# Six of eight output tiles of the last down-projection group as three seven-product pairs, and two changes of order around them

## The chip, the cores and the metric

The kernel runs on one core of a Trainium2 chip. The metric is the time of one execution on the device in microseconds; of several executions the median is given. Five engines work beside each other, each through its own queue in order: PE (TensorE, matmuls; its weight loads are listed as PEld), DVE (VectorE), ACT (ScalarE), POOL (GpSimd; here it issues DMAs that add while they copy) and SP (SyncE, which issues the ordinary DMAs).

## The reference

One decoder layer over 512 tokens of width 1024: an RMS norm, one wide input projection, a pooling mixer and a sparse attention whose results are merged by gates, an output projection with a residual, then a second norm and a gated feed-forward part. What the change touches, cut to the core:

```python
blk = kv[:, idx] + pe[None, None, :, None, :]           # compression: windows of 32 tokens
hid = silu(einsum('bnlgd,ldh->bngh', blk, w1))
...
h = rms_norm(x, ffn_norm_g)                              # x: (1, 512, 1024)
gate_pre, val = split(h @ w_up, 2)                       # D_FF = 2816 = 22 blocks of 128
gate_c = causal_dwconv(gate_pre, conv_w, conv_b)         # width 3 along the tokens
x = x + (silu(gate_c) * val) @ w_down                    # y @ w_down, y: (512, 2816)
```

All is float32. The output is `x`, kept as eight tiles of 128 features by 512 tokens.

## The kernel before

**Precision.** A float32 matrix is split into a high part that PE takes in its fast format (`fp32r`) and the rest. A product is three matmuls: high by high, high by low, low by high. `mm3` (line 451) does this with 512 token columns, one unit of three matmuls per block of 128 of the contraction. The splits are ACT conversions and DVE subtractions (`split`), or, in `split_by_dma` (line 1112), two ACT conversions and a POOL DMA that adds.

**Feed-forward.** The up projection runs over 22 blocks `f`. In blocks 0 and 2 (`up_plain`) gate and value are two plain products of 8 units. The other 20 (`up_fast`, line 1246) compute gate and value together: with weights and tokens each cut in two halves, a two by two block product is made by seven half products (`product`, line 1196: 4 units of three matmuls with 256 columns) in place of eight. The sums of weight halves (`r1`, `r2`, `s3`, and sums in place in `wraw`) are made by DVE and split again; the sums of the tokens' halves (`th`, `tl`) are made once. The last two products of a block, for `h5` and `h4`, are held back and stand inside the next block. When they end, DVE and ACT make the block's gate, its convolution and `y`, and `split_y` splits `y` into `yh`, `yl`.

**Down projection.** It sums over the 22 blocks of `y`. Blocks 0 to 15 are four groups of four (`dn_group`); each group gives eight tiles of 12 matmuls, which are added to `x2`. These `dn` tiles stand between the up products where the table `FILL` (lines 56 to 58) says: an entry gives, for block `f`, how many stand before it and at three places in it. Groups become available at blocks 5, 9, 13 and 17 (`AT`). Blocks 16 to 21 of `y` are the last group, called `dz` here after its weights `wdz`: a loop over eight output tiles (line 1329), 6 units each, whose result plus `x2` is stored. The eighth tile is made as two halves of 256 columns.

**Compression.** `kv_in` (line 747) projects the inputs and DVE makes two tensors `kcb` by adding the position parameters. A `behind` at line 756 holds these additions until `turned[3]`, the last step of transposing queries and keys (`k`), has been done. PE then multiplies `kcb` with `w1`.

**Order.** The code doesn't issue instructions; it records them, and a planner (`Plan.run`, line 226; `emit`, line 375) writes an order for each engine. PE's work comes in two streams, each in its written order: the main line and, until the attention ends, a second one of projections, taken when the main line isn't ready. For the other engines the planner picks among what is ready by due times, which it works out back from PE. It tries several orders and keeps the one that it prices lowest. So an edit anywhere can reorder every queue. SBUF pages of 128x512 (`page`, 54 of them) and the three slots of each ring (`wraw`, `whi`, `wlo`) are handed on from user to user; a tile made by `soon` takes its page in the written order. Since all instructions leave through the planner, all have the line 394 in the profile, and are told apart by tiles: `mm`, `tr`, `av`, `sc` are the accumulator banks.

Of the kernel before, what the change touches and what calls it, by code (L numbers as in the profile page):

```python
# [9 lines left out]
F32R = mybir.dt.float32r  # L10
I32 = mybir.dt.int32
AF = mybir.ActivationFunctionType
# [3 lines left out]
P = 128  # L16
# [38 lines left out]
AT = (5, 9, 13, 17)  # L55
FILL = {f: (0, 0, 0, 0) for f in range(22)}
FILL.update({f: (0, 1, 1, 0) for f in range(5, 18)})
FILL.update({18: (0, 1, 0, 0), 19: (0, 1, 0, 0), 20: (0, 1, 0, 0), 21: (0, 1, 0, 0)})
TRIES = 12
RESERVE = 3  # L60
BASE = 5.0
# [336 lines left out]
def hybrid_layer(ctx: ExitStack, tc: tile.TileContext, xT, pos, par, cst, poolw, w1, wa, wb, wf,  # L398
# [15 lines left out]
    def soon(name, dt=F32):  # L414
        t = page(name, dt=dt)
        pl.early[t.tensor.name] = len(pl.early)
        return t
# [7 lines left out]
    def split(dst_hi, dst_lo, src, scale=None):  # L425
        if scale is None:
            ACT.activation(dst_hi, src, AF.Copy)
            DVE.tensor_sub(dst_lo, src, f32(dst_hi))
        else:
            ACT.activation(dst_hi, src, AF.Copy, scale=scale)  # L430
            DVE.scalar_tensor_tensor(dst_lo, src, scale, f32(dst_hi), op0=ALU.mult, op1=ALU.subtract)

    def ring(name, dt=F32):
        return pl.tile(sb, (P, 1024), dt, name, name, RINGS[name])
# [13 lines left out]
    def flat(ap):  # L448
        return ap.rearrange("p k n -> p (k n)")
# [252 lines left out]
    def qk_transpose(t):  # L702
        pt = bank("tr", (P, 4, P))
        with pl.unit():
            for i in range(4):
                PE.transpose(pt[:, i], qp[t][:, 2 * i:2 * i + 2].rearrange("p a d -> p (a d)"), ident)
        for a in range(2):
            QT[a, t] = page("qt", (P, 4, P), F32R)
            halves_of(pt, QT[a, t], QT[a, t], a)
        if t % 2:  # L710
            pt = bank("tr", (P, 2, 2, P))
            with pl.unit():
                for j in range(2):
                    for b in range(2):
                        PE.transpose(pt[:, j, b], kp[t - 1 + j][:, 2 * b:2 * b + 2].rearrange("p a d -> p (a d)"), ident)
            for g in range(2):
                x, y = (page("kt", (P, 2, 2, P), F32R) for _ in range(2))
                KT[g, t // 2, g], KT[1 - g, t // 2, g] = x, y
                r, o = halves_of(pt, x, x, g)
                ACT.activation(y[o], pt[r], AF.Copy)  # L720
                ACT.activation(y[r], f32(x[o]), AF.Copy)

    rotate(0)
    rotate(1)
    turned = []
    for t in range(NT):
        qk_transpose(t)
        turned.append(pl.last())
# [17 lines left out]
    with pl.on("f"):  # L746
        def kv_in(i):
            pt = feature(i, xh, xl)
            kc = page("kc", (P, 2, 256))
            for g in range(2):  # L750
                for q in range(2):
                    DVE.tensor_mul(kc[q * 64:(q + 1) * 64, g], pt[g * 64:(g + 1) * 64, q::2],
                                   rb[g * 64:(g + 1) * 64, q::2])
            for a in range(2):
                b = page("kcb", (P, 2, 32, 8))
                with pl.behind(turned[3]):
                    DVE.tensor_add(b.rearrange("p g n l -> p (g n) l"), kc.rearrange("p g (n l) -> p (g n) l", l=8),
                                   pe[:, i, 8 * a:8 * a + 8][:, None, :].to_broadcast([P, 64, 8]))
                KC[i, a] = b
# [314 lines left out]
    def any_bank():  # L1074
        turn[0] += 1
        return bank(("mm", "tr", "tr", "mm", "tr", "av")[turn[0] % 6])
# [35 lines left out]
    def split_by_dma(hi, lo, x):  # L1112
        ACT.activation(lo, x, AF.Copy, scale=-1.0)
        POOL.dma_start(lo, x, accum_op=ALU.add)
        ACT.activation(hi, x, AF.Copy)
# [42 lines left out]
    def conv(f, g, pg):  # L1158
# [4 lines left out]
        ACT.activation(t, t, AF.Silu)  # L1163
        return t

    def split_y(f, y):
        yh[f], yl[f] = page("yh", dt=F32R), page("yl", dt=F32R)
        split(yh[f], yl[f], y)

    def up_plain(f):  # L1170
        pts = []
# [20 lines left out]
    def back(x):  # L1192
        n = x.ap[1][1]
        return bass.AP(tensor=x.tensor, offset=x.offset + n - 1, ap=[list(x.ap[0]), [-1, n]])

    def product(bank_, a, b, k0):
        ah, al = a
        bh, bl = b
        for k in range(4):
            c = slice(k * P, (k + 1) * P)  # L1200
            with pl.unit():
                for j, (w, x) in enumerate(((ah, bh), (ah, bl), (al, bh))):
                    PE.matmul(back(bank_[:, :H2]), w[:, c], back(x(k)), start=k0 and k == 0 and j == 0,
                              stop=k == 3 and j == 2, skip_group_check=True)

    def mov(i, half):
        if i == 0:
# [35 lines left out]
            for a in range(2):  # L1243
                fills.append(lambda free, c=c, a=a: one(c, a, free))

    def up_fast(f, n1, n2, n3):
        rg, r1, r2 = ring("wraw"), soon("r1"), soon("r2")
        SP.dma_start(rg, flat(wup[f, 0]))
        with pl.behind(begun[-2 - max(0, 3 - f)]):
            SP.dma_start(r1, flat(wup[f, 1, :, 0:4]))  # L1250
            SP.dma_start(r2, flat(wup[f, 1, :, 4:8]))

        def pair():
            return soon("sh", F32R), soon("sl", F32R)

        def summed(x):
            lo, hi = soon("sl", F32R), soon("sh", F32R)
            split_by_dma(hi, lo, x)
            return hi, lo

        a1 = ring("whi", F32R), ring("wlo", F32R)
        split(*a1, rg)
        halves_ = lambda a, i: tuple(q[:, i * 512:(i + 1) * 512] for q in a)
        s3 = soon("s3")
        DVE.tensor_add(s3, rg[:, :512], r1)
        h5 = summed(r2)
        DVE.tensor_add(r1, r1, r2)
        h3 = summed(s3)
        DVE.tensor_add(rg[:, :512], rg[:, :512], r1)
        h1 = summed(r1)  # L1270
        h2 = pair()
        split(*h2, rg[:, :512])
        DVE.tensor_add(rg[:, 512:], rg[:, 512:], rg[:, :512])
        h4 = summed(rg[:, 512:])
        bx, by, bq = any_bank(), any_bank(), any_bank()
        half = [page("u1")]
        u2, u3 = half[0][:, :H2], half[0][:, H2:]
        g, y = page("fg"), page("y")
        product(bx, halves_(a1, 0), mov(0, 0), True)
        begun.append(pl.last())  # L1280
        ACT.activation(by[:, :H2], bx[:, :H2], AF.Copy)
        more = list(held)
        del held[:]
        if more:
            more[0]()
        else:
            product(bq, h1, mov(2, 0), True)
        fill(n1)
        product(by, h2, mov(2, 1), False)
        ACT.activation(u2, by[:, :H2], AF.Copy)  # L1290
        if more:
            more[1]()
        fill(n3)
        if more:
            product(bq, h1, mov(2, 0), True)
        product(bx, halves_(a1, 1), mov(1, 0), False)
        DVE.tensor_mul(g[:, :H2], bx[:, :H2], rb[:, :H2])
        fill(n2)
        product(by, h3, mov(3, 0), False)
        ACT.activation(u3, by[:, :H2], AF.Copy)  # L1300
        DVE.tensor_add(y[:, H2:], bq[:, :H2], u3)
        DVE.tensor_mul(y[:, H2:], y[:, H2:], rb[:, H2:])

        def end1():
            product(by, h5, mov(3, 1), False)
            DVE.tensor_mul(y[:, :H2], by[:, :H2], rb[:, :H2])

        def end2():
            product(bq, h4, mov(1, 1), False)
            DVE.tensor_add(g[:, H2:], bq[:, :H2], u2)  # L1310
            DVE.tensor_mul(g[:, H2:], g[:, H2:], rb[:, H2:])
            t = conv(f, g, g)
            DVE.scalar_tensor_tensor(y, y, -1.0, t, op0=ALU.mult, op1=ALU.mult)
            split_y(f, y)

        held.extend((end1, end2))
# [9 lines left out]
    fill(1, True)  # L1326
    finish()
    fill(9, True)
    for f in range(8):
        wh, wl = weights(flat(wdz[f]), 768, "v")  # L1330
        pt = any_bank()
        o = page("o")
        if f < 7:
            mm3(pt, wh, wl, yh, yl, 16, KF, koff=16, nk=KF, first=16)
            DVE.tensor_add(o, pt, x2[f])
            SP.dma_start(out[f], o)
            continue
        for h in range(2):
            s = slice(h * H2, (h + 1) * H2)
            pt = any_bank() if h else pt  # L1340
            for k in range(16, KF):
                c = slice((k - 16) * P, (k - 15) * P)
                with pl.unit():
                    for j, (w, q) in enumerate(((wh, yh), (wh, yl), (wl, yh))):
                        PE.matmul(back(pt[:, :H2]), w[:, c], back(q[k][:, s]), start=k == 16 and j == 0,
                                  stop=k == KF - 1 and j == 2)
            DVE.tensor_add(o[:, s], pt[:, :H2], x2[f][:, s])
            SP.dma_start(out[f, :, s], o[:, s])

    pl.emit(TRIES, RESERVE)  # L1350

# [92 lines left out]
```

## Time and profile before

| | |
|---|---|
| median of 3 runs | 691.0 us (690.94 to 691.12) |
| the profiled execution | 690.67 us |
| its span, first to last instruction | 688.9 us |
| granted TensorE clock | 1.000 |
| PE, DVE, ACT, POOL busy | 683.1, 502.6, 430.0, 100.2 us |
| DMA | 113.99 MB, mean 165 GB/s |

In a row of the chain stand start, length, engine, accumulator bank and the count of merged instructions, in microseconds from the start of the span. In a row of the timeline the operation is written output<-inputs, with the shape; a bracket gives the idle time before it and what ended it. A row of the groups gives busy time and mean nanoseconds of one, then idle time before and what ended most of it.

### The profile page before, as it was taken

Reading aid. Unit: us, or ns where it says so; the run is one execution under the profiler, and the core shown is the slowest. Engines: PE = TensorE matmul, PEld = TensorE weight load, DVE = VectorE, ACT = ScalarE, POOL = GpSimd, SP = SyncE. Lnnn points to the kernel's source line nnn. Section 1 sums busy time; section 2 is a strip of 40 time slices with the busy share of each in tenths; the row PEclk is TensorE's granted clock in tenths of the full one; section 3 lists DMA queues with packets and bytes.
Section 4 is the critical chain, followed back from the end, with each engine's and each line's share of the span. In section 5 each row is a group of like instructions: output and inputs, shape, how many; then the busy total and the mean of one; then the engine's idle time right before and its main releaser. Section 6 shows DMA issues by size and latency. Waiting matters only on the chain.

```text
span 688.9 us, 11345 instructions
## 1 busy us (share of the span) xinstructions
PE 683.1 (99%) x4126; PEld 606.0 (88%) x4126; DVE 502.6 (73%) x1093; ACT 430.0 (62%) x781; POOL 100.2 (15%) x126
## 2 busy tenths in 40 slices
PE   9999999999999999999999999999999999999997
PEld 8898888888888888888898999999999999999976
DVE  6868678887877644768868978677778777786642
ACT  7667477776776653346778866666567656675320
POOL 0011210111111110001123332122213222211000
PEclk9999999999999999999999999999999999999999
DMA  8468653545545557844778889677668667765131
GB/s 301 143 165 264 154 121 94 139 100 145 154 123 154 153 138 246 279 148 154 209 167 221 199 180 218 154 199 184 153 170 185 170 157 194 170 167 115 47 130 61
DMA packets 46279, 113.99 MB, mean 165 GB/s; under 512 B 5392, under 2 KB 6160, under 8 KB 46224
## 3 DMA queue, kind: packets, MB, share of 16 engines
q1 hardware_dynamic: 29808, 76.43, 32.5%
q0 software_dynamic: 16128, 36.71, 29.9%
q8 instruction: 32, 0.52, 0.3%
q14 instruction: 23, 0.19, 0.1%
q10 hardware_dynamic: 288, 0.14, 0.1%
HBM read 70.27 MB, written 6.29 MB: 111 GB/s over the span
## 4 chain that ended last, share of the span: by engine, by line
PE 97%; DVE 1%; DMA 1%; ACT 0%; issue 0%; SPq 0%
PE mm L394 37%; PE tr L394 33%; PE sc L394 16%; PE av L394 11%; DMA wraw<-wa 1%; ACT kt L394 0%; DVE ft L394 0%; DVE fg L394 0%; DVE wlo L394 0%; ACT ft L394 0%; SPq L394 0%; DVE yl L394 0%; DVE kcb L394 0%; DVE u L394 0%; DVE kt L394 0%
## 5 line engine op out<-in xcount | busy, mean ns | idle before, releaser
L394 ACT ACTIVATE whi<-wraw 128x1024 fp32r<-128x1024 f32 (+2 forms) x94 | 95.2, 1015 | 65.8 <-PE mm L394 26.7
L394 DVE TENSOR_TENSOR wlo<-wraw,whi 128x1024 fp32r<-128x1024 f32 (+1 forms) x66 | 76.2, 1156 | 4.6 <-ACT whi L394 4.2
L394 PE MATMUL mm<-xh,whi 128*128 128x512 f32 x176 | 72.3, 411 | 0.1
L394 PE MATMUL tr<-tl,sh 128*128 128x256 f32 x250 | 70.4, 282 | 0.0
L394 PE MATMUL mm<-xh,wlo 128*128 128x512 f32 x176 | 68.9, 392 | 0.0
L394 PE MATMUL mm<-xl,whi 128*128 128x512 f32 x176 | 68.9, 391 | 0.0
L394 PE MATMUL tr<-th,sl 128*128 128x256 f32 x240 | 67.7, 282 | 0.0
L394 PE MATMUL tr<-th,sh 128*128 128x256 f32 x240 | 67.5, 281 | 0.0
L394 PE MATMUL mm<-gh,whi 128*128 128x256 f32 (+1 forms) x320 | 60.8, 288 | 0.0
L394 POOL DMA_DIRECT2D wlo<-wraw x28 | 24.3, 867 | 238.3 <-ACT wlo L394 182.0
L394 POOL DMA_DIRECT2D sl<-r x40 | 34.5, 862 | 134.2 <-ACT sl L394 98.0
L394 PEld LDWEIGHTS mm<-gh,whi 128*128 128x128 f32 x320 | 49.5, 188 | 0.6
L394 PEld LDWEIGHTS tr<-tl,sh 128*128 128x128 f32 x250 | 47.0, 188 | 0.5
L394 PE MATMUL sc<-yh,whi 128*128 128x512 f32 x120 | 46.7, 389 | 0.0
L394 PE MATMUL sc<-yl,whi 128*128 128x512 f32 x120 | 46.7, 389 | 0.0
L394 PE MATMUL sc<-yh,wlo 128*128 128x512 f32 x120 | 46.7, 389 | 0.0
L394 PEld LDWEIGHTS tr<-th,sh 128*128 128x128 f32 x240 | 45.2, 188 | 1.2
L394 PE MATMUL mm<-gh,wlo 128*128 128x256 f32 (+1 forms) x160 | 45.9, 287 | 0.0
L394 PEld LDWEIGHTS tr<-th,sl 128*128 128x128 f32 x240 | 45.1, 188 | 0.0
L394 DVE SCALAR_TENSOR_TENSOR ft<-fg,pr,ft 128x511 f32<-128x511 f32 (+1 forms) x44 | 32.9, 749 | 14.3 <-ACT ft L394 13.7
L394 PEld LDWEIGHTS mm<-xh,wlo 128*128 128x128 f32 x176 | 33.0, 188 | 7.5
L394 ACT ACTIVATE u<-tr 128x256 f32<-128x256 f32 x40 | 15.3, 384 | 36.8 <-PE tr L394 24.2
(380 smaller groups left out, 1927.2 us busy)
## 6 DMA issues: line engine op xcount, KB each, us to landing
wlo<-wraw POOLq DMA_DIRECT2D x28, 512.0 KB, 4.7
wraw<-wup SPq DMA_DIRECT2D x24, 512.0 KB, 3.6
wraw<-wf SPq DMA_DIRECT2D x22, 512.0 KB, 3.4
r<-wup SPq DMA_DIRECT2D x40, 256.0 KB, 3.5
sl<-r POOLq DMA_DIRECT2D x40, 256.0 KB, 4.0
wraw<-wdn SPq DMA_DIRECT2D x16, 512.0 KB, 3.7
sl<-s POOLq DMA_DIRECT2D x20, 256.0 KB, 4.3
sl<-wraw POOLq DMA_DIRECT2D x20, 256.0 KB, 4.3
```

The lines of the kernel that those rows point to most:

```text
L394: getattr(self.real[o.eng], method)(*a, **kw)
```

## The change

1. `FILL` loses the `dn` tile inside each of blocks 19, 20 and 21. The tiles left over then stand after block 21: as before one ahead of its two held products, and now four behind them in place of one.
2. In `kv_in` the additions wait for `flipped[1]`, the last transposition of `k` on PE, and not for the copies that follow it.
3. The weight preparation of `up_fast` becomes a function `half_weights` with a width and a choice which sums are split by DMA; `up_fast` calls it with its old width and choices.
4. Six `dz` tiles are made in pairs (`dz_fast`): two output tiles `f`, `e`, the contraction cut into blocks 16 to 18 and 19 to 21, the tokens into two halves; seven products of 3 units with 256 columns. The sums of `y` (`y_sums`) are made as blocks 19, 20 and 21 of `y` become ready, from each of them and the block three before. Two tiles stay plain and come first. The half-width results are added to `x2` and stored as halves.

```diff
-FILL.update({18: (0, 1, 0, 0), 19: (0, 1, 0, 0), 20: (0, 1, 0, 0), 21: (0, 1, 0, 0)})
+FILL.update({18: (0, 1, 0, 0), 19: (0, 0, 0, 0), 20: (0, 0, 0, 0), 21: (0, 0, 0, 0)})
...
+            flipped.append(pl.last())
...
-                with pl.behind(turned[3]):
+                with pl.behind(flipped[1]):
...
+    def y_sums(k):
+        b1, b2 = ylast[k], ylast[k + 3]
+        ta, tb = page("ta"), page("tb")
+        DVE.tensor_sub(ta[:, :H2], b1[:, :H2], b1[:, H2:])
+        DVE.tensor_sub(tb[:, :H2], b2[:, H2:], b1[:, H2:])
+        DVE.scalar_tensor_tensor(ta[:, H2:], ta[:, :H2], -1.0, b2[:, H2:], op0=ALU.mult, op1=ALU.subtract)
+        DVE.scalar_tensor_tensor(tb[:, H2:], ta[:, H2:], -1.0, b2[:, :H2], op0=ALU.mult, op1=ALU.subtract)
+        for i, x in ((0, ta), (1, tb)):
+            yth[k - 16, i], ytl[k - 16, i] = page("yth", dt=F32R), page("ytl", dt=F32R)
+            split(yth[k - 16, i], ytl[k - 16, i], x)
...
+    def half_weights(first, second, w, dma, gate):
+        rg, r1, r2 = ring("wraw"), soon("r1"), soon("r2")
+        SP.dma_start(rg[:, :2 * w], first)
+        with pl.behind(gate):
+            SP.dma_start(r1[:, :w], second[0])
+            SP.dma_start(r2[:, :w], second[1])
...
+        a1 = tuple(ring(n, F32R)[:, :2 * w] for n in ("whi", "wlo"))
+        split(*a1, rg)
+        s3 = soon("s3")[:, :w]
+        DVE.tensor_add(s3, rg[:, :w], r1)
+        h5 = parts(r2, dma[0])
+        DVE.tensor_add(r1, r1, r2)
+        h3 = parts(s3, dma[1])
+        DVE.tensor_add(rg[:, :w], rg[:, :w], r1)
+        h1 = parts(r1, dma[2])
+        h2 = parts(rg[:, :w], dma[3])
+        DVE.tensor_add(rg[:, w:], rg[:, w:], rg[:, :w])
+        h4 = parts(rg[:, w:], dma[4])
...
-    for f in range(8):
...
+    DZ = (True, True, False, False, True)
+
+    def dz_fast(f, e):
+        L, Rr = slice(0, H2), slice(H2, T)
+        a11, a12, h1, h2, h3, h4, h5 = half_weights(flat(wdz[f]), (flat(wdz[e, :, 0:3]), flat(wdz[e, :, 3:6])), 384,
+                                                    DZ, begun[-4])
+        bx, by, bq = any_bank(), any_bank(), any_bank()
+        of, oe = page("o"), page("o")
+        product(bx, a11, ymov(0, 0), True, 3)
+        begun.append(pl.last())
+        ACT.activation(by[:, L], bx[:, L], AF.Copy)
+        product(bq, h1, ymov(2, 0), True, 3)
+        DVE.tensor_sub(oe[:, Rr], x2[e][:, Rr], bq[:, L])
+        product(by, h2, ymov(2, 1), False, 3)
+        DVE.tensor_add(of[:, Rr], by[:, L], x2[f][:, Rr])
+        product(bx, a12, ymov(1, 0), False, 3)
+        DVE.tensor_add(of[:, L], bx[:, L], x2[f][:, L])
+        SP.dma_start(out[f, :, L], of[:, L])
+        product(by, h3, ymov(3, 0), False, 3)
+        DVE.tensor_sub(oe[:, Rr], oe[:, Rr], by[:, L])
+        SP.dma_start(out[e, :, Rr], oe[:, Rr])
+        product(bq, h4, ymov(1, 1), False, 3)
+        DVE.tensor_add(of[:, Rr], of[:, Rr], bq[:, L])
+        SP.dma_start(out[f, :, Rr], of[:, Rr])
+        product(by, h5, ymov(3, 1), False, 3)
+        DVE.tensor_sub(oe[:, L], x2[e][:, L], by[:, L])
+        SP.dma_start(out[e, :, L], oe[:, L])
+
+    for f in range(2):
+        dz_plain(f)
+    for f in range(2, 8, 2):
+        dz_fast(f, f + 1)
```

`parts(x, by_dma)` splits a sum by `split_by_dma` where the flag is set and by `split` where it isn't; `dz_plain` is the old loop's body for a whole tile; `ymov` picks a half of `yh`, `yl` or of the sums.

More of the change, by code (lines that the diff above doesn't have):

```diff
@@ L724, in hybrid_layer @@
     rotate(1)
-    turned = []
+    turned, flipped = [], []
     for t in range(NT):
@@ L1164, in conv @@
         return t
+    yth, ytl, ylast = {}, {}, {}
+    def y_sums(k):
[8 more added lines that the diff above has]
+            split(yth[k - 16, i], ytl[k - 16, i], x)
     def split_y(f, y):
@@ L1168, in split_y @@
         split(yh[f], yl[f], y)
+        if f > 15:
+            ylast[f] = y
+        if f > 18:
+            y_sums(f - 3)
     def up_plain(f):
@@ L1194, in back, with product @@
         return bass.AP(tensor=x.tensor, offset=x.offset + n - 1, ap=[list(x.ap[0]), [-1, n]])
-    def product(bank_, a, b, k0):
+    def product(bank_, a, b, k0, n=4):
         ah, al = a
         bh, bl = b
-        for k in range(4):
+        for k in range(n):
             c = slice(k * P, (k + 1) * P)
@@ L1203, in product @@
                     PE.matmul(back(bank_[:, :H2]), w[:, c], back(x(k)), start=k0 and k == 0 and j == 0,
-                              stop=k == 3 and j == 2, skip_group_check=True)
+                              stop=k == n - 1 and j == 2, skip_group_check=True)
     def mov(i, half):
@@ L1244, in dn_group, with parts @@
                 fills.append(lambda free, c=c, a=a: one(c, a, free))
-    def up_fast(f, n1, n2, n3):
[L1247 to L1274, printed above, removed]
+    def half_weights(first, second, w, dma, gate):
[4 more added lines that the diff above has]
+            SP.dma_start(r2[:, :w], second[1])
+        rg, r1, r2 = rg[:, :2 * w], r1[:, :w], r2[:, :w]
+        def parts(x, by_dma):
+            if by_dma:
+                lo, hi = soon("sl", F32R)[:, :w], soon("sh", F32R)[:, :w]
+                split_by_dma(hi, lo, x)
+            else:
+                hi, lo = soon("sh", F32R)[:, :w], soon("sl", F32R)[:, :w]
+                split(hi, lo, x)
+            return hi, lo
+        a1 = tuple(ring(n, F32R)[:, :2 * w] for n in ("whi", "wlo"))
[10 more added lines that the diff above has]
+        h4 = parts(rg[:, w:], dma[4])
+        return tuple(q[:, :w] for q in a1), tuple(q[:, w:] for q in a1), h1, h2, h3, h4, h5
@@ L1275, in up_fast @@
+    def up_fast(f, n1, n2, n3):
+        a11, a12, h1, h2, h3, h4, h5 = half_weights(flat(wup[f, 0]), (flat(wup[f, 1, :, 0:4]), flat(wup[f, 1, :, 4:8])),
+                                                    512, (True, True, True, False, True), begun[-2 - max(0, 3 - f)])
         bx, by, bq = any_bank(), any_bank(), any_bank()
@@ L1278, in up_fast @@
         g, y = page("fg"), page("y")
-        product(bx, halves_(a1, 0), mov(0, 0), True)
+        product(bx, a11, mov(0, 0), True)
         begun.append(pl.last())
@@ L1295, in up_fast @@
             product(bq, h1, mov(2, 0), True)
-        product(bx, halves_(a1, 1), mov(1, 0), False)
+        product(bx, a12, mov(1, 0), False)
         DVE.tensor_mul(g[:, :H2], bx[:, :H2], rb[:, :H2])
@@ L1328, in hybrid_layer, with ymov, dz_plain @@
     fill(9, True)
-    for f in range(8):
+    def ymov(i, half):
+        c = slice(half * H2, (half + 1) * H2)
+        if i < 2:
+            return tuple((lambda k, q=q: q[16 + 3 * i + k][:, c]) for q in (yh, yl))
+        return tuple((lambda k, q=q: q[k, i - 2][:, c]) for q in (yth, ytl))
+    def dz_plain(f):
         wh, wl = weights(flat(wdz[f]), 768, "v")
@@ L1332, in hybrid_layer @@
         o = page("o")
[L1333 to L1348, printed above, removed]
+        mm3(pt, wh, wl, yh, yl, 16, KF, koff=16, nk=KF, first=16)
@@ new lines, in dz_plain @@
+        begun.append(pl.last())
+        DVE.tensor_add(o, pt, x2[f])
+        SP.dma_start(out[f], o)
+    DZ = (True, True, False, False, True)
[6 more added lines that the diff above has]
+        product(bx, a11, ymov(0, 0), True, 3)
+        begun.append(pl.last())
+        ACT.activation(by[:, L], bx[:, L], AF.Copy)
[15 more added lines that the diff above has]
+        SP.dma_start(out[e, :, L], oe[:, L])
```

## The prediction

> **What bounds the kernel now.** I read the page's busy shares and its chain first, then what the tensor engine waits for, then the chain and the timeline of the stretches that the change touches.
>
> ```profile
> span 688.9 us, 11345 instructions
> PE 683.1 (99%) x4126; PEld 606.0 (88%) x4126; DVE 502.6 (73%) x1093; ACT 430.0 (62%) x781; POOL 100.2 (15%) x126
> PE 97%; DVE 1%; DMA 1%; ACT 0%; issue 0%; SPq 0%
> ```
> ```profile
> PE mm L394 <- POOL ones L394: 1.0, 1, 1.0
> PE tr L394 <- DVE kcb L394: 0.6, 1, 0.6
> PE tr L394 <- ACT xh L394: 0.3, 1, 0.3
> PE av L394 <- DVE yl L394: 0.2, 1, 0.2
> ```
>
> Columns of the second fence: waiter, what it waited for, microseconds, times, longest. PE is the bound almost everywhere and waits four times in all. So a change gains only by less PE work, or at one of these four waits; it loses by any wait that it creates. Two of the four lie where the change works: `kcb` (compression) and `yl` (the last `y`).
>
> The price of PE work is a distance from start to start, since matmuls overlap (a 256-column matmul lasts 0.28 us but starts every 0.12). The chain shows it (start, length, what, matmuls):
>
> ```profile
> 621.00 2.72 PE sc L394 x12
> ...
> 642.06 1.42 PE tr L394 x12
> 643.48 2.72 PE mm L394 x12
> 646.20 2.85 PE tr L394 x24
> ...
> 655.89 0.73 PE av L394 x2
> 656.63 4.09 PE mm L394 x18
> 660.72 8.16 PE tr L394 x36
> ...
> 681.12 2.13 PE mm L394 x18
> 683.25 2.15 PE tr L394 x18
> ```
>
> Twelve matmuls of 512 columns (a `dn` tile) take 2.72, 0.227 each; twelve of 256 (a half product) 1.42, 0.118 each. A `dz` tile is 18 of 512: 4.08. The last tile, cut in two, costs 2.13 + 2.15.
>
> **Part 1: half products.** Six `dz` tiles cost now 5 x 4.08 + 2.13 + 2.15 = 24.68. After, three pairs of seven products of nine 256-column matmuls: a product is 9 x 0.118 = 1.065, a pair 7.455, three 22.37. Gain 2.31. The tail behind the last matmul (add of a 256-column half, a 128 KB store) is the same kind as now: 0.
>
> On the other engines a pair prepares weights 384 wide, an unseen width; its neighbours:
>
> ```profile
> L394 DVE TENSOR_TENSOR wlo<-wraw,whi 128x768 fp32r<-128x768 f32 x16 | 15.2, 955 | 1.2 <-ACT whi L394 1.2
> L394 DVE TENSOR_TENSOR r<-r,r 128x512 f32<-128x512 f32 x20 | 13.7, 687 | 0.3
> L394 DVE TENSOR_TENSOR y<-y,rb 128x256 f32<-128x256 f32 x20 | 8.3, 416 | 0.0
> L394 ACT ACTIVATE whi<-wraw 128x768 fp32r<-128x768 f32 x15 | 12.5, 843 | 24.7 <-PE mm L394 7.5 <-PE tr L394 7.2 <-PE sc L394 5.4
> L394 ACT ACTIVATE sl<-r 128x512 fp32r<-128x512 f32 x40 | 24.8, 620 | 0.0
> L394 ACT ACTIVATE tr<-mm 128x256 f32<-128x256 f32 x19 | 7.0, 368 | 7.0 <-PE mm L394 7.0
> L394 POOL DMA_DIRECT2D sl<-r x40 | 34.5, 862 | 134.2 <-ACT sl L394 98.0 <-DVE ft L394 12.8 <-PE sc L394 7.3
> ```
>
> At 384 I take the middle, 0.55 on DVE (between 0.416 and 0.687) and 0.5 on ACT (between 0.368 and 0.620). DVE per pair: 0.955 + six x 0.55 + six half-width results x 0.42 = 6.8 (5.9 to 7.6 with the ends). ACT: 0.843 + eight x 0.5 + one copy 0.37 = 5.2. POOL: three x 0.86 = 2.6. All under or at the pair's 7.455, and the first pair is prepared under `dn` and `dz` tiles, where these engines idle. So PE stays the bound. If DVE took 7.6, two pairs would lose 0.15 each.
>
> Inside a pair a product often continues a bank whose contents DVE or ACT must first read or copy, with one product, 1.065, between: 0.42 for the read leaves about 0.6. If the read must queue behind one 768-wide subtraction (0.955), PE waits about 0.3. There are three such joints per pair, nine in all: 0 to 2.7. I take 0: in the built order, what DVE does between two such reads fits between them (the closest, 0.42 + 0.55 after a read, ends 0.1 before the next bank is complete), and ACT's copy in the first pair stands behind a 0.843 conversion that can start 1.065 earlier, when the second plain tile ends.
>
> Transfers: the bytes are those of before (384 KB per tile), and three 192 KB accumulations per pair are new.
>
> ```profile
> sl<-r POOLq DMA_DIRECT2D x40, 256.0 KB, 4.0
> wraw<-wdz SPq DMA_DIRECT2D x8, 384.0 KB, 3.1
> ```
>
> In SP's order the loads of the last pair's second tile stand behind the stores of the two plain tiles. DVE makes the later of these adds only after its first bank read in the first pair, about 3.2 into that pair (three products); so these loads go out about 4 into it and land some 3.1 later, before the second pair begins (7.455). The third pair begins 7.455 after that, and their chain (two adds, a conversion, an accumulation of 4.0, about 6) fits. Cost 0. If it did not, PE would wait as long as it is late; bound 0 to 1.
>
> **Part 2: the `y` sums.** For each of three tile pairs DVE makes four half-width operations and two 512-wide subtractions, 4 x 0.42 + 2 x 0.69 = 3.06, ACT two conversions, 1.24. In the order nearly all of it stands behind the preparation of the last up pair's weights, then under `dn` tiles, `dz` tiles and the first pair. 0, as long as part 3's pairs hold.
>
> **Part 3: three `dn` tiles leave the up pairs 19, 20, 21** (the group's last five now stand one ahead of the last two half products and four behind them; now it is one and one). PE's work is only moved. Their adds move along, and so do their two 512 KB loads on SP, which go behind the loads of pairs 20 and 21; a set whose first half pair 18 uses keeps one of three ring slots until all pairs are done. By the order, pair 21's wide conversion then waits for pair 19's last use of its slot, a pair's length before its need: 0. What is lost is a cover: 2.72 in each pair. Pairs without such a tile stand earlier in the trace:
>
> ```profile
> 373.02 1.42 PE mm L394 x12
> ...
> 382.96 1.42 PE mm L394 x12
> ...
> 392.90 1.42 PE mm L394 x12
> ```
> ```profile
> 373.02:382.96 9.94, 9.94 (x86) 9.94 (x86) 9.06 (x15) 8.27 (x15) 3.45 (x4) 1.00 0.87 204
> 608.34:621.00 12.66, 12.66 (x97) 12.19 (x97) 10.74 (x18) 8.29 (x16) 2.40 (x3) 1.00 0.61 159
> ```
>
> (Window, length, then busy PE, weight loads, DVE, ACT, POOL; clock; DMA share; GB/s.) They run 9.94 apart, exactly seven products, with DVE busy 9.06 of it: no wait, but little room. After the change pairs 19 to 21 are such pairs, with three pages of `y` and the new sums held besides. By the order the tightest item is the low part of pair 21's second weight sum: its page comes free when pair 20's last product ends, 2.84 before it is used, and needs 0.69 plus DVE's queue (one 1024-wide subtraction and two short ones, about 1.6). Cost 0, room about 0.5 to 1.3.
>
> What this buys is the wait for the last `y`. From 651.60 the first `dz` tile runs until 656.47 in PE's timeline:
>
> ```profile
> 651.60 0.39 PE L394 MATMUL av<-yh,whi 128*128 128x512 f32 x1
> ...
> 655.89 0.50 PE L394 MATMUL av<-yl,whi 128*128 128x512 f32 x1 [0.23 <-DVE yl L394]
> ...
> 656.47 0.39 PE L394 MATMUL mm<-yh,whi 128*128 128x512 f32 x1
> ```
>
> That is 4.87 for 4.08: 0.79 lost, more than the 0.2 that the waits view books. Now one `dn` tile, 2.72, and the tile's first 15 matmuls, 3.4, lie between the last half product and the need of `yl`; after, four tiles, 10.9, and 3.4. The `y` chain took 655.89 - 649.05 (the end of the group at 646.20) = 6.8. Gain 0.79, or 0.2 if the waits view were all of it.
>
> **Part 4: compression.** DVE's two `kcb` additions no longer wait for the last copy of `k`.
>
> ```profile
> 70.81 0.60 PE L394 MATMUL tr<-cs,kp 128*128 128x128 f32 x4
> ...
> 73.29 0.69 DVE L394 TENSOR_TENSOR qt<-tr,qt 64x512 fp32r<-64x512 f32 x1
> 73.77 0.39 PE L394 MATMUL mm<-xh,wlo 128*128 128x512 f32 x1
> 74.00 0.63 ACT L394 ACTIVATE kt<-kt 64x512 fp32r<-64x512 f32 x1
> 74.00 1.29 DVE L394 TENSOR_TENSOR kcb<-kc,pr 128x512 f32<-128x512 f32 x2
> 74.75 1.50 PE L394 MATMUL tr<-kcb,w 128*128 128x62 f32 x11 [0.59 <-DVE kcb L394]
> ```
>
> PE starts 0.98 after a matmul that needs 0.23: 0.75 lost. After, the transposes of `k` (done by 71.4) free the additions, and a subtraction of `k` steps behind them; behind two `qt` subtractions of 0.69 they would end near 73.2, before PE asks at 74.0. Gain 0.75, between 0 (PE meets the next late weight) and 0.75.
>
> **The rest.** The planner writes a new order everywhere. PE's stays almost the same; in the first loads an activation tile now goes ahead of the second weights, which PE needs only in its second round. I take 0, with -0.3 to +1.5 as bounds: waits as long as the longest of before, twice.
>
> **Sum.** 2.31 + 0.79 + 0.75 = 3.85. The profiled execution took 690.67 us (688.9 span), 0.3 under the median of 691.0; so 686.8 for such an execution and 687.1 for the median.
>
> **Rivals.**
> A. *Joints or new order cost something.* Half of the joints' 2.7 and one new wait of 1: 2.3 lost, 689.4. For it: DVE at 6.8 of 7.455 in the pairs. Against: pairs 373 to 393, DVE fuller, without a wait.
> B. *The up pairs needed their covers* (slower). If preparing a pair's weights still takes the 12.66 of a pair with a tile, PE waits 2.72 in each of pairs 19, 20, 21: 8.2 lost, 695.4. It decides from a loss of 3.85 + 1.4 = 5.2, a preparation of 11.7 per pair. For it: three `y` and the sums take pages from the weights. Against: 9.94 without a wait at 373 to 393.
> C. *Half-width matmuls cost more than half.* Break-even is 24.68 / 189 = 0.131 each; 0.146 would make the kernel slower by 1.4. If each paid the weight load openly, 0.188 by its row below, the three pairs would take 35.5, and the time is 700.3. Against: in the window at 373 the loads are busy 9.94 of 9.94 already, so the 0.118 holds the load.
>
> ```profile
> L394 PEld LDWEIGHTS tr<-th,sh 128*128 128x128 f32 x240 | 45.2, 188 | 1.2
> ```
>
> [...]
>
> D. *Nothing moves:* the two waits come back elsewhere and the joints take the products' gain; 690.7.
>
> **Chances and range.** Forecast 0.62, A 0.20, D 0.10, B 0.06, C 0.02. A change under 0.2%, 1.4 us, can't be told from none: same from 689.6 to 692.4. Forecast and most of A are faster, D and a bit of A the same, B and C slower: 0.80, 0.12, 0.08. Range 686.5 (the early-order gain of 0.3, rounding) to 690.0, which holds the forecast and A; the forecast's own is 686.5 to 688.3.
>
> **What would show it.** In the new profile: no wait for `kcb` and none for `yl`; the last stretch as two groups of 18 at 4.08 and 21 products of 9 at 1.07; pairs 19 to 21 at 9.94; PE's waits about 1.3 in all. Wrong would show as waits of `mm`, `tr` or `av` for DVE or ACT `o`, for `sl` or `sh`, or 9-matmul products longer than 1.1.

## The result, and the profile after

The changed kernel took 689.2 us (median of 12 executions, 687.97 to 690.34) beside 691.1 for the kernel before (13 executions, the main body of them 690.5 to 691.5); the ratio is 0.9959, 95% interval 0.9942 to 0.9975. By the ratio it is faster by 0.41%, 2.8 us, where the forecast was 3.9. Measured again beside other kernels it took 688.43 (11 executions, 687.04 to 691.14), ratio 0.9966, interval 0.9949 to 0.9984. The sign and the range held. The forecast of 687.1 is reached by none of the first 12 executions and by one of the second 11: the changed kernel spreads over 2.4 and 4.1 us where the main body of the kernel before spreads over 1.0 and 2.1 beside it, and the spread is what had to be explained.

Some executions of the kernel before (20 of 87 in these comparisons are over 692 us, most of them near 694.4) are longer than the rest, and one of the changed kernel, 1133.58 us at a granted clock of 0.556, is left out of all figures here. The ratios are not quotients of the medians: the first one, 0.9959, equals the quotient of the means with the four long executions of before in it. Without these four the medians differ by 1.95 us and the means by 1.8, so that an ordinary execution gained about half of the forecast in the first group and 1.9 to 2.4 us in the second.

The profiled execution is one of the longest, 690.34 us. The page's first part and its chain:

```profile
span 688.5 us, 11627 instructions
PE 680.9 (99%) x4189; PEld 607.7 (88%) x4189; DVE 518.3 (75%) x1137; ACT 442.9 (64%) x811; POOL 108.1 (16%) x135
PE 91%; DMA 4%; ACT 2%; DVE 1%; issue 1%; SPq 0%; ACTq 0%; POOLq 0%; DVEq 0%
```

PE is busy 2.2 us less than before, yet its span is only 0.4 shorter, and DMA and ACT stand in the chain with 4% and 2% (1% and 0% before). What PE waits for, in the columns of the prediction:

```profile
PE tr L394 <- ACT u L394: 1.9, 2, 1.5
PE mm L394 <- POOL ones L394: 1.0, 1, 1.0
PE tr L394 <- DVE qp L394: 0.6, 1, 0.6
PE tr L394 <- DVE sl L394: 0.5, 1, 0.5
```

`kcb` and `yl` are gone as forecast, and `xh` as well; three new ones stand in their place. With `ones`, which stays, PE waits 4.0 in all, where it waited 2.1 before and the prediction expected about 1.3. The 2.3 less of products and the 1.9 more of waits make the 0.4. The end, in the chain (start, length, what, matmuls), is as forecast:

```profile
658.57 4.08 PE mm L394 x18
662.65 1.06 PE tr L394 x9
663.71 1.06 PE mm L394 x9
...
683.95 1.08 PE av L394 x9
685.03 0.02 issue
685.05 0.42 DVE o L394
```

From 662.65 to 685.03 stand 21 products in 22.4 us, 1.065 each, with no wait at a joint.

The longest new wait lies in the up projection, in a stretch that the change doesn't touch. The chain there:

```profile
514.17 8.09 DMA sl<-r
...
522.32 5.19 DMA r<-wup
...
532.42 1.04 ACT whi L394
533.46 0.28 ACT u L394
533.73 0.04 issue
533.77 1.69 PE tr L394 x12
```

Read it upwards. PE started at 533.77, late by 1.51, because ACT copied `u` late; ACT was behind because it had stood until 527.6 for the load `r<-wup`; that load went out at 522.32 because its page was still being read by an accumulating transfer `sl<-r`, which took 8.09 us. What waits for loads of this kind between 440 and 620 us (in the kernel before nothing does):

```profile
ACT sl L394 <- DMA r<-wup: 10.4, 3, 4.7
DVE s L394 <- DMA r<-wup: 4.2, 3, 2.7
DVE r L394 <- DMA r<-wup: 3.6, 2, 2.1
```

A pair loads two such tiles, `r1` and `r2`; a row of SP's timeline spans both, so its length shows how much later the second went out. Before, and then after, at the same pair:

```profile
517.28 1.74 SPq L394 DMA_DIRECT2D r<-wup  x2
```
```profile
517.66 4.99 SPq L394 DMA_DIRECT2D r<-wup  x2
```

The built programs say why. Pairs are counted here in the order in which they are made, from 1; blocks 0 and 2 are plain, so the 14th pair is block 15. The second load of this pair waits for PE before, and for an accumulating transfer (`DMASW`) after:

```
before: DMACopy r_1246<-wup 128x512 [waits DMAHW7_49,PE_49]
after:  DMACopy r_1246<-wup 128x512 [waits DMAHW3_49,DMAHW7_49,DMASW0_49,DVE_49]
```

By its address it takes in the first the page of an `sh`, last read by PE, and in the second the page of the 13th pair's own `r2`, which POOL's transfer reads. The wait for this transfer is new in pairs 10, 14 and 18 (the load of pair 18 waited before for another accumulating transfer).

That comes from the planner's choice. It makes twelve orders; numbers 2 and 3 are planned as if each transfer landed 1.2 us late, numbers 4 and 5 as if 2.0 (`LANDS`, line 65 after). For the kernel before it keeps number 5, for the changed kernel number 2. With the compression edit alone it keeps 2 as well, without that edit 5.

### The profile page after: what moved, and what is told of

Its sections match the earlier page's. It is cut to its first block, busy times and chain, and to the rows that moved or that the text cites. A ratio compares the mean times of both kernels' runs of the same rounds, so it can differ in the third digit from the quotient of the medians.

```text
span 688.5 us, 11627 instructions
## 1 busy us (share of the span) xinstructions
PE 680.9 (99%) x4189; PEld 607.7 (88%) x4189; DVE 518.3 (75%) x1137; ACT 442.9 (64%) x811; POOL 108.1 (16%) x135
## 4 chain that ended last, share of the span: by engine, by line
PE 91%; DMA 4%; ACT 2%; DVE 1%; issue 1%; SPq 0%; ACTq 0%; POOLq 0%; DVEq 0%
PE mm L394 35%; PE tr L394 32%; PE sc L394 13%; PE av L394 11%; DMA r<-wup 2%; DMA sl<-r 1%; DMA w<-w 1%; ACT whi L394 1%; DMA xr<-xT 0%; ACT sh L394 0%; ACT ft L394 0%; ACT kt L394 0%; ACT sl L394 0%; DVE qp L394 0%; DVE qt L394 0%
## 5 line engine op out<-in xcount | busy, mean ns | idle before, releaser
L394 ACT ACTIVATE whi<-wraw 128x1024 fp32r<-128x1024 f32 (+2 forms) x91 | 92.7, 1019 | 41.2 <-PE mm L394 20.4
L394 DVE TENSOR_TENSOR wlo<-wraw,whi 128x1024 fp32r<-128x1024 f32 (+1 forms) x63 | 73.3, 1165 | 5.3 <-ACT whi L394 4.5
L394 POOL DMA_DIRECT2D sl<-r x43 | 37.1, 862 | 165.1 <-ACT sl L394 99.5
L394 PE MATMUL sc<-yh,whi 128*128 128x512 f32 x108 | 42.1, 389 | 0.0
L394 PE MATMUL sc<-yl,whi 128*128 128x512 f32 x108 | 42.0, 389 | 0.0
L394 PE MATMUL sc<-yh,wlo 128*128 128x512 f32 x108 | 42.0, 389 | 0.0
L394 ACT ACTIVATE wlo<-wraw 128x1024 fp32r<-128x1024 f32 x28 | 29.7, 1061 | 15.5 <-PE mm L394 12.9
```

Source lines behind the costliest of these rows:

```text
L394: getattr(self.real[o.eng], method)(*a, **kw)
```

## The experiments

Medians in us, with lowest, highest and number of executions; the kernel before beside each group had 691.1, 691.1, 690.8 and 690.9.

| kernel | order | median (range, n) | ratio to before (95%) |
|---|---|---|---|
| changed kernel | 2 | 689.2 (687.97–690.34, 12) | 0.9959 (0.9942–0.9975) |
| all_order5 | 5 | 687.79 (687.37–688.23, 6) | 0.9947 (0.9933–0.9962) |
| no_compression | 5 | 688.31 (687.85–688.79, 6) | 0.9955 (0.9940–0.9970) |
| compression_only | 2 | 692.93 (689.36–695.74, 12) | 1.0014 (0.9994–1.0033) |
| before_order2 | 2 | 692.62 (690.81–695.13, 12) | 1.0021 (1.0008–1.0035) |
| handoff_back | 5 | 688.52 (687.53–689.53, 12) | 0.9960 (0.9947–0.9974) |
| dn_alone | 5 | 690.87 (689.55–693.81, 12) | 1.0002 (0.9983–1.0022) |
| products_alone | 5 | 688.74 (688.16–692.58, 12) | 0.9977 (0.9958–0.9996) |
| compression_alone5 | 5 | 690.62 (689.82–691.43, 12) | 0.9978 (0.9961–0.9994) |
| handoff_freed | 2 | 688.40 (687.98–688.59, 5) | 0.9967 (0.9955–0.9979) |
| after_again | 2 | 688.43 (687.04–691.14, 11) | 0.9966 (0.9949–0.9984) |
| all_order5_again | 5 | 688.01 (687.33–688.47, 5) | 0.9961 (0.9949–0.9973) |
| four_pairs5 | 5 | 688.03 (686.64–688.73, 6) | 0.9958 (0.9945–0.9971) |

### Is it the order? The same change in order 5, the same old kernel in order 2

`all_order5` is the changed kernel and `before_order2` the kernel before, each with one line of `emit` changed:

```diff
-            if best is None or spans < best[0]:
+            if i == 5:
```

(`i == 2` in `before_order2`.)

> The whole change, but the planner is made to keep its sixth order (number 5, planned with transfers that land late; the kernel before has its order from there too) instead of the third (number 2), which it kept for the changed kernel. In number 5 the second 256 KB load of pairs 10, 14 and 18 doesn't wait for an accumulating transfer. Theory 1 (the missing 2 us are waits for loads that this order of pages makes late, and that come and go with the transfers): 687.1, at most 688.2 if compression gains nothing in this order, all runs within 1.0 of each other, no wait of PE for u between 440 and 600. Theory 2 (the order of the up pairs doesn't matter, the loss is in the tail: sums of y, pair 21): 689.2, spread 2 as before.

> The kernel before, nothing edited but that the planner keeps order number 2 instead of number 5. Theory 1: between 691.1 and 693.3, median near 692.5, a spread over 1.5, waits of PE for u in single profiles. Theory 2: 691.1, narrow.

Both came out as theory 1 says, but that `before_order2` reaches up to 695.13 where at most 693.3 was expected. Order 2 alone costs the kernel before 1.5 us in the median and spreads it over 4.3; order 5 alone takes the changed kernel to 687.79, spread 0.9. The waits of PE in `all_order5`, and its row of the 14th pair's loads:

```profile
PE mm L394 <- POOL ones L394: 1.0, 1, 1.0
PE mm L394 <- DVE u L394: 0.3, 1, 0.3
PE tr L394 <- DVE pp L394: 0.2, 1, 0.2
```
```profile
517.53 1.78 SPq L394 DMA_DIRECT2D r<-wup  x2
```

The loads go out 1.78 apart again, and neither ACT `u` nor `sl` holds PE. (The `u` of DVE here is another tile, at 127 us.)

### Which edit brings the order? Without the compression edit, and with it alone

```diff
-                with pl.behind(flipped[1]):
+                with pl.behind(turned[3]):
```

`no_compression` is the changed kernel with this line; `compression_only` is the kernel before with the opposite of it. The latter has one more wait turned from `turned[3]` to `flipped[1]`, that of POOL's zeroing of `pz` (line 993), which the changed kernel leaves as it was; so it isn't the compression edit quite alone. The planner chose for itself.

> The change without its compression edit: the additions wait for the copies of k again. By itself this brings the planner back to order number 5. Theory 1: 691.1 - 2.31 - 0.79 = 688.0, so 1.2 under the whole change although it lacks an edit that was to gain 0.75; narrow runs. Theory 2: 689.2 + 0.75 = 690.0, or 689.2 if that edit gains nothing.

> The kernel before with the compression edit alone; the planner then keeps order number 2, with the page hand-offs of the changed kernel. Theory 1: 690.4 in the best runs, and up to 2.2 more in others, median 691 to 692.5, a spread over 1.5. Theory 2: 690.4, narrow, or 691.1 if the wait only moves.

Theory 1 again. The change is 0.9 quicker *without* the edit that was to gain 0.75 (0.1 against the second group of the changed kernel), and `compression_only` is slower than the old kernel in the median, by more than theory 1 had said (692.93, where 692.5 was the upper end; its ratio, 0.9994 to 1.0033, is not clear of 1). Beside `before_order2`, which has order 2 without the edit, it is the same (692.93 and 692.62): the order costs, not the edit. In its profiled execution (694.99 us) PE waits at the 14th pair too, in PE's timeline:

```profile
533.98 0.39 PE L394 MATMUL tr<-th,sh 128*128 128x256 f32 x1 [1.73 <-ACT u L394]
```

The wait is 1.73 long, where the changed kernel's profile had 1.51.

### Is it the page hand-off? Put into order 5, and taken out of order 2

Both kernels hold an order fixed by a list of its instructions. `handoff_back` is the whole change in order 5:

```diff
-        rg, r1, r2 = ring("wraw"), soon("r1"), soon("r2")
+        rg, r1 = ring("wraw"), soon("r1")
+        r2 = older[0] if again else soon("r2")
+        older[:] = [r2]
```

with `again` true in pairs 10, 14 and 18. `handoff_freed` is the changed kernel in order 2, with `r2 = cs[:, 128:640]` in the same three pairs, a stretch of constants that the attention has finished with. Both edits also shift which pages later tiles get: beside the three loads, 8 other instructions of `handoff_back` and 48 of `handoff_freed` wait for another set of engines or queues in the built programs. So neither isolates the hand-off entirely.

> The whole change in order number 5, held fixed instruction for instruction; but the second 256 KB load of pairs 10, 14 and 18 is put into the page of the pair before's second load, as order number 2 does by its choice of pages, so that it waits for the accumulating transfer that reads this page. Nothing else changes. Theory 1a (it is this hand-off that costs): between 687.8 and 690, median 688.4 to 689.8, a spread over 1.2, DVE or ACT waiting for r<-wup again near 520 and 585 us. Theory 1b (order number 2 loses by something else, this hand-off is hidden): 687.8, narrow.

> The changed kernel in its own order number 2, held fixed instruction for instruction; only the second 256 KB loads of pairs 10, 14 and 18 land in a stretch of the constants' tile that nobody reads any more, so that they don't wait for the accumulating transfer of the pair before. Theory 1a (this hand-off is what order number 2 loses by): 687.6 to 688.4, spread under 1.2, no PE wait for u near 533 and 596 us. Theory 1c (the order itself asks for the loads too early, the hand-off is only half of it): 688.3 to 689.2, with DVE and ACT still waiting for r<-wup. Theory 1b (the hand-off is hidden): 689.2, spread 2.4.

> The changed kernel once more, beside the others on one chip, for a second profile. 689.2, a spread of 2.4; PE waits for u near 533 or 596 us and for sl near 631 us, of other lengths than in the first profile.

> The whole change in order number 5 once more, beside the others on one chip. 687.8, spread 0.9; no wait for u between 440 and 600 us.

`handoff_freed` lost the spread: 0.6 us in 5 executions, where the same order with the hand-off, on the same chip, spread over 4.1 in 11. Between 440 and 620 us the waits for the second loads are (in `after_again`, then in `handoff_freed`, where the loaded tile is called `cs`):

```profile
ACT sl L394 <- DMA r<-wup: 11.2, 4, 3.7
DVE r L394 <- DMA r<-wup: 6.1, 5, 1.7
DVE s L394 <- DMA r<-wup: 2.5, 3, 1.4
```
```profile
DVE s L387 <- DMA r<-wup: 1.8, 3, 1.0
ACT sl L387 <- DMA cs<-wup: 1.5, 2, 1.2
```

PE no longer waits for `u`. So the hand-off probably makes the late executions, those over 688.6 (5 of the 11 of `after_again`, none of these 5, which are few). It doesn't account for the median of that session, 688.40 against 688.43, and the median fits theory 1c as well as 1a. What `handoff_freed` still has of order 2 are the waits for `qp` (0.6) and `sl` (0.5). Its waits of PE are 2.1 in all; those of `all_order5_again` are 1.5, and its median is 0.4 lower.

`handoff_back` shows the other half. The loads are as late as in order 2, but nearly nothing waits for them:

```profile
518.04 5.05 SPq L387 DMA_DIRECT2D r<-wup  x2
```
```profile
ACT sl L387 <- DMA r<-wup: 1.6, 1, 1.6
DVE r L387 <- DMA r<-wup: 0.9, 1, 0.9
```

Its profile has no wait of PE in the up projection. Its executions spread over 2.0, but so does the main body of the kernel before beside it (689.43 to 691.46), so that this spread is no sign of the hand-off. By these profiles a late load costs where the order also asks for it early, and order 2 does both; this rests on one profile of `handoff_back`, and is argued from it rather than shown. How much of handoff_back's 0.5 to 0.7 over `all_order5` is the hand-off and how much the session (two different groups) stays open.

### What each part is worth alone

`dn_alone` is the kernel before with the new `FILL`; `products_alone` the changed kernel with the old `FILL` and `turned[3]`; `compression_alone5` the kernel before with `flipped[1]`. All three with `if i == 5:`. (`compression_alone5` also has the changed wait of `pz`.)

> The kernel before with the six dz tiles as seven half products per pair (and the sums of y), the dn tiles and the compression left as they were, in order number 5. Part 1 of the prediction: 691.1 - 2.31 = 688.8; if joints or the sums of y under the old dn tiles cost something, 689 to 690.5, with waits of PE in the last 30 us.

> The kernel before with the three dn tiles moved behind pair 21, nothing else, in order number 5. Part 3 of the prediction: 691.1 - 0.79 = 690.3, no wait for yl, none in pairs 19 to 21. If these pairs needed their covers: over 691.1.

> The kernel before with the compression edit alone, kept in order number 5. Part 4 of the prediction: 691.1 - 0.75 = 690.35, narrow. If the wait only moves to the next late operand: 691.1.

Without the upper group of each (four of `products_alone` from 691.45, five of `dn_alone` from 692.25, none of `compression_alone5`, eight of before's 35 from 692.49), the medians are 688.25, 690.26 and 690.62, beside 690.62 for before. So by medians the products gain 2.37, the moved tiles 0.36, the compression edit nothing. The products are as priced. The 0.36 isn't clear of the noise: these seven executions of `dn_alone` lie between 689.55 and 691.05, and with 692.25, whose granted clock is an ordinary 0.999, the median is 690.44 and the gain 0.18. Its profile says more. The wait for `yl` is gone, pairs 19 to 21 (blocks, as in the prediction) have none, and the first `dz` tile takes 4.08 where it took 4.87; its 693.37 us less 3.4 us lost at half clock (last section) are 690.0, 0.7 under the 690.67 of before's profile. These are one profile each. So the mechanism held, and the size stays open between 0.2 and 0.7.

For the compression edit there is a second pair of kernels in order 5, `no_compression` and `all_order5`, which differ by this edit alone: 688.31 and 687.79 in one group of six executions each, 0.5 in favour of the edit, though the ranges overlap and both profiled executions took 688.1. So it gains 0 to 0.5 in order 5. It exchanges one wait for others there: `kcb` 0.6 is gone and `u` 0.3 and `pp` 0.2 are new (the fence of `all_order5` above). In order 2 the wait for `kcb` is replaced by one 8 us earlier, for `qp`. That belongs to the order and not to the edit, for the old kernel in order 2, which lacks the edit, has it too. PE's timeline in the changed kernel, then in `before_order2`:

```profile
66.91 0.63 PE L394 MATMUL tr<-cs,qp 128*128 128x128 f32 x4 [0.61 <-DVE qp L394]
```
```profile
67.51 0.63 PE L394 MATMUL tr<-cs,qp 128*128 128x128 f32 x4 [0.61 <-DVE qp L394]
```

### A larger step

`four_pairs5` makes all eight `dz` tiles in pairs, in order 5:

```diff
-    for f in range(2):
-        dz_plain(f)
-    for f in range(2, 8, 2):
+    for f in range(0, 8, 2):
```

> All eight dz tiles as four pairs, no plain tile, in order number 5. By the product's price of 1.065: 2 x 4.08 - 7.455 = 0.70 less, 687.1. Against it: the first pair's second product needs the last sums of y 6.3 us earlier (its first product is 1.07 long, the plain tiles 8.16 less their first 3.4); if they are late by a part of that, PE waits for ta or yth and the gain is gone, 687.8 to 689.

It gained nothing that can be told: 688.03 beside 688.01. PE didn't wait for the sums of `y`, against which the expectation warned. A joint was late, at 674.74, and three earlier products take 1.12 to 1.34 instead of 1.07 in the chain (at 662.12, 664.46 and 666.86); the row of PE's waits:

```profile
PE mm L394 <- DVE o L394: 0.4, 1, 0.4
```

Here the cover of one product that the prediction counted for the joints was not always enough. The best version of all runs is thus the change in order 5: 687.79 and 688.01, ratios 0.9947 and 0.9961.

## Why the prediction was right, and where it was off

- **Part 1, half products: right.** 21 products of 1.065, 22.4 us, no late joint; alone 2.37 for 2.31. (In the profile of `products_alone` one joint is late, by 0.24 at 674.23.) Rival C is out, for a matmul took 0.118 (1.065 / 9) where break-even was 0.131.
- **Part 2, sums of `y`: off.** That "nearly all of it stands behind the preparation of the last up pair's weights" was true but for one operation, and in order 2 that one counted. In the changed kernel DVE stood 2.01 us for the page of `ta`, which an accumulating transfer still held; the rows of DVE's timeline:

```profile
626.59 0.43 DVE L394 TENSOR_TENSOR ta<-y 128x256 f32<-128x256 f32 x1 [2.01 <-DMA sl<-r]
...
628.71 1.22 DVE L394 TENSOR_TENSOR wlo<-wraw,whi 128x1024 fp32r<-128x1024 f32 x1
...
630.18 0.69 DVE L394 TENSOR_TENSOR sl<-wraw,sh 128x512 fp32r<-128x512 f32 x1
```

- **Part 3, moved tiles: mechanism right, size open.** No wait for `yl`. The "tightest item", the low part of pair 21's second weight sum, was named rightly, but its room of 0.5 to 1.3 was too large: it is the `sl` of 630.18, and PE waited 0.53 for it, as DVE's queue had been held by `ta`. In two more profiles of order 2 the one follows the other: in `handoff_freed` `ta` waited 1.91 and PE 0.55, in `after_again` `ta` 0.49 and PE not at all. In order 5 `ta` doesn't wait, and PE has no wait for `sl` in its list; in `all_order5` its weight load still waits 0.19 for it, so the room was none. Alone the move gained 0.2 to 0.7 for 0.79. Rival B is out: in the profile of `dn_alone` pairs 19 to 21 run without their covers and PE doesn't wait.
- **Part 4, compression: wrong in size.** The wait for `kcb` went; all of it was taken as gained. The lower end of 0, "PE meets the next late weight", is nearer to what happened: in order 5 `u` and `pp`, 0.5 of new waits for 0.6, and 0 to 0.5 gained in the medians. In order 2 it is `qp`, with or without the edit.
- **The rest: the step that failed.** "I take 0, with -0.3 to +1.5." The kernel before was quieter because it had another order, which happens to be one planned for late transfers. One small edit made the planner keep order 2, and that costs by execution between nothing (687.04) and about 4 us (691.14), in the median 1.4 between the first groups in which each order of the change ran (689.2 against 687.79) and 0.4 where both ran in one group (688.43 against 688.01). In the kernel before, where both orders ran in one group, it costs 1.5. Rival A's number, 689.4, was nearly met by this half of it, the new order; its joints were not. That the stated range held is owed to its having been drawn to take in rival A.

The sum with what was measured in order 5, 2.37 + 0.2 to 0.7 + 0 to 0.5, is 2.6 to 3.6; the two groups gave 3.1 (687.79 from 690.91, the median of before's executions under 692) and 2.8 (688.01 from 690.83).

## What to carry to other kernels

Where a planner writes the order, the price of an edit includes the order that it tips the planner into: compare which of its candidates it kept, and for what landing times, before pricing the rest at zero. A page handed from an accumulating transfer to a load puts two transfers in a row (8.09 and 5.19 us at the 14th pair of the changed kernel); in the profiles here nothing of PE's time went where the users of the load stood late in their queues (`handoff_back`), and up to 1.7 us at one pair where they stood early. When a wait is to be removed, look for the next late operand before counting all of it as gained: here 0.5 of new waits stood against 0.6.

## What was not expected of the hardware

**The granted clock can halve after a short wait.** In the profiled execution of `compression_only` the wait of 1.73 us above ended at 533.98. In its windows the clock (the column behind the busy times) is then:

```profile
532.00:534.60 2.60, 0.87 (x8) 0.67 (x7) 2.31 (x4) 2.60 (x6) 1.17 (x2) 1.00 0.74 88
534.60:534.90 0.30, 0.30 (x4) 0.30 (x3) 0.30 (x2) 0.30 (x2) 0.00 (x0) 0.58 0.71 239
534.90:538.00 3.10, 3.10 (x12) 2.71 (x12) 3.07 (x8) 2.15 (x4) 0.41 (x1) 0.50 0.91 247
538.00:538.30 0.30, 0.30 (x3) 0.26 (x2) 0.30 (x1) 0.00 (x0) 0.30 (x1) 0.90 0.07 7
```

The row of 534.90 has 0.50, half clock. With the rows beside it taken as part full and part half, what is missing from 1.00 in the last three rows, divided by a half, is 0.25 + 3.10 + 0.06 = 3.4 us at half clock, 1.7 us lost behind the wait itself (an estimate from these rows). After the wait of 1.51 in the changed kernel the clock stayed at 1.00 (533.77 to 541.00). In that of `dn_alone` (693.37 us) a wait of 0.59 for `kcb`, with 32 narrow matmuls behind it, was followed by half clock:

```profile
73.00:76.80 3.80, 3.21 (x22) 2.63 (x21) 3.70 (x7) 3.01 (x5) 0.46 (x1) 1.00 0.71 264
76.80:77.40 0.60, 0.60 (x8) 0.60 (x7) 0.57 (x2) 0.60 (x1) 0.60 (x3) 1.00 0.00 0
77.40:84.20 6.80, 6.80 (x25) 5.84 (x25) 4.50 (x9) 1.58 (x4) 1.85 (x7) 0.52 0.66 157
84.20:84.60 0.40, 0.40 (x3) 0.30 (x2) 0.00 (x0) 0.00 (x0) 0.00 (x0) 0.63 0.00 0
```

By the same working it is 6.5 + 0.3 = 6.8 us at half clock, 3.4 us lost. The wait alone doesn't decide it. The profile of the kernel before, an ordinary execution, has the same wait of 0.59 and the same 32 matmuls, and its clock stays:

```profile
77.40:84.20 6.80, 6.80 (x50) 6.31 (x50) 4.20 (x9) 1.25 (x3) 1.52 (x6) 1.00 0.63 157
```

The 3.4 us are the distance between the two groups of times of the kernel before. Its long executions also show it in their mean granted clock: where it was taken, it is 0.995 in all 13 executions over 694 us and 0.999 to 1.000 in the ordinary ones, and 0.005 of 690 us is 3.4. (Three between 692.4 and 693.3 have 0.998.) With this `kcb` wait in place, 20 of 87 executions of before, 4 of 12 of `dn_alone` and 4 of 12 of `products_alone` (none of 6 of `no_compression`) lie in such an upper group; without it, in order 5, none of 41. The late executions of order 2 are of another kind: in `before_order2` the clock is 0.999 to 1.000 up to 695.13 us. So the compression edit, worth 0 to 0.5 in an ordinary execution, probably removes these long ones; where in the kernel before the clock was lost was not seen, as no long execution of it was profiled.

The half clock lasted 3.4 us behind a wait of 1.73 in `compression_only` and 6.8 us behind one of 0.59 in `dn_alone`. What besides the wait is needed stays open.

**An accumulating transfer can take nearly twice its median.** The one of 514.17, of 256 KB, landed after 8.09 us in the changed kernel, where the median of these transfers (`sl<-r`) is 4.4 over the whole span and the prediction reckoned with 4.0. A 512 KB load, a 256 KB load and three more accumulations were issued within these 8 us, another 512 KB load 0.6 us ahead of them, and the DMA share was 1.01 to 1.11 in the windows from 518 to 524. That these transfers slowed it is not shown.
